# A hybrid diffusion layer on one core: constant matmuls ahead of the first ff tile, PSUM sums copied by ScalarE, weight loads released one by one, lo parts last

## The chip, the cores and the metric

The kernel runs on one core of a Trainium2 chip. The metric is device time in microseconds (us). A core has TensorE for matmuls (PE in the profile; its weight loads are PEld), VectorE (DVE), ScalarE (ACT), GpSimd (POOL) and SyncE (SP). Loads from HBM are asked for by instructions on a queue, SP's, POOL's or ACT's, and are carried by 16 DMA engines.

## The reference

One layer over 256 latent tokens and 256 context tokens of width 2048: a half-step SwiGLU, a mixing step (grouped-query attention beside a Hyena long convolution), and a second half-step SwiGLU for the latent tokens. Each is RMS-normed and modulated by a linear map of the conditioning vectors.

```python
mod = (s_lat @ w_ada[l] + b_ada[l])[:, None, :]          # 9 chunks of 2048; s = silu(c)
mod_c = (s_ctx @ w_ada[l] + b_ada[l])[:, None, :]        # the same for the context
def half_ffn(s, m, slot, g, w_up, w_down):
    h = rms_norm(s, g) * (1 + chunk(m, 3*slot + 1)) + chunk(m, 3*slot)
    return s + 0.5 * chunk(m, 3*slot + 2) * swiglu(h, w_up, w_down)
x = half_ffn(x, mod, 0, g_norm[l, 0], w_ffn1_up[l], w_ffn1_down[l])        # and ctx with mod_c
...
h = (h @ w4).reshape(L, 2, HYENA_WIDTH) * exp(-t * abs(decay))             # the Hyena filter's taps
kk = concat([h[:, 0], zeros, h[:0:-1, 1]]); kk = kk / sum(abs(kk), axis=0)
x = x + chunk(mod, 5) * merge_groups(attention(...), hyena(..., kk), g_out[l], w_out[l])
x = half_ffn(x, mod, 2, g_norm[l, 2], w_ffn2_up[l], w_ffn2_down[l])
```

## The kernel before

Everything is kept transposed: a tile holds 128 of the 2048 channels (KT = 16 such d) by 256 tokens, latent and context side by side (i = 0, 1), so one matmul has 512 columns. For precision each factor is split into a hi part (a cast to fp32r by ScalarE) and a lo part (what the cast lost, by VectorE), and a product takes three matmuls: whi with the input's hi, whi with its lo, wlo with its hi (`mm3`, L232 to L234; L221 and L225 make the weights' parts).

The change lies in the first 165 us. There three ff tiles (WAVE = 3, j = 0 to 2) are summed up at the same time, channel block by channel block, because the modulation of block d is only just being made. For each d:

- `row_on(d + 1)`, `ada_row` (L175): row sums of w_ada for block d + 1, 32 small matmuls in four column groups over two wrow tiles of 1 MB (the halves kh). A row block's tiles are loaded on SP's queue by `row_load` (L162), two blocks ahead; four buffers hold them.
- `ada_col` (L182 to L190): ScalarE copies the sums out of their PSUM bank (L182), TensorE transposes them (L184), VectorE reduces them to columns of scale and shift, `mod` (L187 to L190).
- `wave_h` (L657 to L661; for d = 0 and 1 `times_rs` and `wave_h_early`, L637 and L644 to L649): normed input times scale plus shift, hi by ScalarE and lo by VectorE.
- the three tiles' matmuls, `f1.tile(d, d % 4, w[j], wave[j])`.
- after d = 3, 7, 11 the next weights: `weights_on` casts raw to whi and wlo (L221, L225). The raw tiles of 512 KB (`raws`, L209) come on POOL's queue.
- one step of `filter_spectrum`, the Hyena filter, a generator that is moved on by one `next(steps)` after each tile. Its four rounds q each load taps on POOL's queue (`load_taps`: L425, L428), make them (L465 to L492), sum their magnitudes (psn: L495, L496; reciprocal L498, middle bin L499) and transform them (L504 to L507). L509 to L512 write the result to DRAM.

The bank of PSUM that a row block, a transform or the sums of magnitudes use comes from one pool of four (`PB`, "pb" in the rows); two of the four hold the third ff tile all through this stage.

Ahead of d = 0 stand the sums of squares of the tokens (L596 and the matmuls of 2 columns), the row sums of block 0 and the spreading of 1/rms over the partitions (row, two matmuls of 512 columns at 21.79 us in the profile). `keep_awake(n)` issues n constant matmuls (ones by a tile of ones, 256 columns, L583) whose result nobody reads: 17 at the start and 5 after the first half of the sums.

A planner lays out each engine's order from the program's order and its own estimates of when operands are ready. `then(x, f, ...)` and `tc.issue_after(x)` hold f behind x in that order. Two places before the change:

```python
gate = G.tensor_copy(warm, mod[0][0][:, d : d + 1])
with tc.issue_after(gate.ins):
    raws = [weight_load(f1.wup[j, d // 4 + 1], (P, 4, 2, P), G) for j in range(WAVE)]
```

Of the kernel before, what the change touches and what calls it, by code (L numbers as in the profile page):

```python
# [18 lines left out]
P = 128  # L19
D = 2048  # L20
KT = D // P
# [10 lines left out]
WAVE = 3  # L32
# [1 line left out]
FILTER_J = 36  # L34
GATE_J = 20

AWAKE = (17, 5)

QSTEP = (2, 1, 3, 2)
FILL = (2, 0)  # L40
# [15 lines left out]
def hybrid_layer_kernel(ctx: ExitStack, tc: tile.TileContext, a):  # L56
    nc = tc.nc
    V, S, G, PE = nc.vector, nc.scalar, nc.gpsimd, nc.tensor
# [56 lines left out]
    mod = [[None] * 9, [None] * 9]  # L115
# [7 lines left out]
    warm = mod[0][8][:, 0:1]  # L123
# [83 lines left out]
    def weight_load(src, shape, queue=None):  # L207
        raw = T(wp, shape, "raw", bufs=4)
        load = (queue or nc.sync).dma_start(raw, src)  # L209
        loads.append(load)  # L210
        if done[0]:
            last_load[0] = load
        return raw
# [38 lines left out]
    def then(behind, do, *args, **kw):  # L252

        with tc.issue_after(behind.ins):
            return do(*args, **kw)
# [87 lines left out]
    class Ffn:  # L343
# [18 lines left out]
        def tile(self, k, k4, w, ps2):  # L362
            for half in range(2):
                mm = self.mm(ps2[half], (w[0][:, k4, half, :], w[1][:, k4, half, :]), self.h[k], k == 0, k == KT - 1)
            return mm

        def close(self, j, ps2):
            sg = tmp2((P, 2, L))
            S.activation(sg, ps2[0], AF.Silu)
            V.tensor_mul(sg, ps2[1], sg)  # L370
            self.acts[j] = split(sg, (P, 2, L))
# [40 lines left out]
    def filter_spectrum():  # L412
# [47 lines left out]
        for q in range(4):  # L460
            now = taps.pop()
            if q < 3:
                taps.append(load_taps(q + 1))
            dec, w4 = now
            S.activation(dec, dec, AF.Abs)  # L465
            kts, pm = [], []
            for t in range(2):
                kts.append(U((P, 2, L)))
                S.activation(kts[t], dec, AF.Exp, scale=tneg[:, t : t + 1])
            whi, wlo = U((P, 2, L), F32R), U((P, 2, L), F32R)  # L470
            S.copy(whi, w4)
            V.tensor_sub(wlo[0:NF], w4[0:NF], whi[0:NF].bitcast(F32))
            yield
            yield
            for t in range(2):
                ps, ht = PB((P, 2, L)), hid[:, t * P : (t + 1) * P]
                PE.matmul(ps, ht, whi, start=True, stop=False)
                PE.matmul(ps, ht[0:NF], wlo[0:NF], start=False, stop=True)
                V.tensor_mul(kts[t], ps, kts[t])
            V.memset(kts[0][0:1, 1, :], 0.0)  # L480
            yield
            for kt in kts:
                pm_ = U((P, 2, L))
                V.tensor_add(pm_[:, 0, :], kt[:, 0, :], kt[:, 1, :])
                V.tensor_sub(pm_[:, 1, :], kt[:, 0, :], kt[:, 1, :])
                pm.append(pm_)
            yield
            for kt in kts:
                S.activation(kt, kt, AF.Abs)
            ab = kts[0][:, 0, :]  # L490
            V.tensor_add(kts[0], kts[0], kts[1])
            V.tensor_add(ab, ab, kts[0][:, 1, :])  # L492
            yield
            psn = PB((P, 2, L))
            PE.matmul(psn[:, 0, :], ones, ab, start=True, stop=True)  # L495
            PE.matmul(psn[0:1, 1, :], alt, pm[0][:, 0, :], start=True, stop=True)  # L496
            rn, mid = T(up, (P, L), "mt", bufs=3), T(up, (1, L), "mt", bufs=3)
            V.reciprocal(rn, psn[:, 0, :])  # L498
            V.tensor_mul(mid, psn[0:1, 1, :], rn[0:1, :])  # L499
            yield  # L500
            for sn in range(2):
                ps, eo, o = PB((P, 2, L)), kts[sn], now[sn]
                for t in range(2):
                    PE.matmul(ps[:, t, :], mats[:, sn, t, :], pm[t][:, sn, :], start=True, stop=True)  # L504
                V.tensor_mul(eo, ps, rn.unsqueeze(1).broadcast_to((P, 2, L)))
                V.tensor_add(o[:, 0, :], eo[:, 0, :], eo[:, 1, :])
                V.tensor_sub(o[:, 1, :], eo[:, sn, :], eo[:, 1 - sn, :])  # L507
                if sn:
                    V.tensor_copy(o[0:1, 0, :], now[0][0:1, 1, :])  # L509
                    V.tensor_copy(now[0][0:1, 1, :], mid)  # L510
                    for n in range(2):
                        nc.gpsimd.dma_start(spec[2 * q + n], now[n])  # L512
                yield
                if not sn:
                    yield
# [38 lines left out]
    f1 = Ffn(a["w_up1"], a["w_dn1"], 0)  # L554
    load = then(load, row_load, 0)

    raws = [T(wp, (P, 4, 2, P), "raw", bufs=4) for _ in range(WAVE)]
    w = {j: tuple(T(wp, (P, 4, 2, P), n, F32R, 3) for n in ("whi", "wlo")) for j in range(WAVE)}
# [17 lines left out]
    def keep_awake(n, behind=None, bank=spin):  # L576

        last = behind
        with ExitStack() as order:
            if behind is not None:  # L580
                order.enter_context(tc.issue_after(behind.ins))
            for _ in range(n):
                last = PE.matmul(bank[:, 0 : 2 * P], ones, pair, start=True, stop=True)  # L583
        return last
# [9 lines left out]
    for n, t in enumerate(xs[0] + xs[1]):  # L594
# [14 lines left out]
        for i, sq in reversed(summed):  # L609
            for tt in range(2):  # L610
                for j in range(2):
                    awake = then(awake, PE.matmul, sums[:, 2 * i + tt, :], sq[:, j, tt * P : (tt + 1) * P], ones[:, 0:2],
                                 start=n == 7 and (tt, j) == (0, 0), stop=sq is acc and n == 15 and (tt, j) == (1, 1))
        summed, last = [], awake
# [2 lines left out]
    root_table(square)  # L617
    vector(V.tensor_scalar, bada1, bada[:, KT : 2 * KT], 1.0, None, ALU.add)
    r_ = token_root(sums, D)
    for half in range(2):  # L620
        last = then(last, ada_row, 0, (half,))

    parts, row = T(up, (P, 2, 4), "mt", F32R, bufs=3), PB((P, 2, L))
    V.tensor_copy(parts[:, 0, :], r_)
# [42 lines left out]
    wave = [f1.open(alt=j >= 2) for j in range(WAVE)]  # L667
# [6 lines left out]
    spread = S.copy(rs, row)  # L674
    with tc.issue_after(scaled.ins):
        copied, turned_, bank = then(spread_last, ada_col, 0)
    with tc.issue_after(copied.ins), tc.issue_after(made_lo.ins):
        shifted, lo_last = wave_h_early(0)

# [17 lines left out]


    scaled = then(lo_last, times_rs, 1, rs)
    mm = f1.tile(0, 0, w[0], wave[0])  # L700
    mm = then(mm, row_on, 1)
    mm = then(mm, f1.tile, 0, 0, w[1], wave[1])
    with tc.issue_after(mm.ins), tc.issue_after(scaled.ins), tc.issue_after(shifted.ins):
        copied, mm, _ = ada_col(1)
# [3 lines left out]
    mm = then(mm, f1.tile, 0, 0, w[2], wave[2])  # L708
# [12 lines left out]
    for d in range(1, KT):  # L721
        if d > 1:
            mm = then(mm, row_on, d + 1) or mm
        for j in range(WAVE):
            mm = then(mm, f1.tile, d, d % 4, w[j], wave[j])
            if d == 1 and j == 0:
                mm = then(mm, row_on, 2)
            if (d, j) != (1, 0):
                next(steps, None)
            if j == (1 if d == 1 else 0):  # L730
                mm = then(mm, col_on, d + 1) or mm
            weights_on(d, j)
        if d % 4 == 1 and d // 4 < 3:
            gate = G.tensor_copy(warm, mod[0][0][:, d : d + 1])
            with tc.issue_after(gate.ins):
                raws = [weight_load(f1.wup[j, d // 4 + 1], (P, 4, 2, P), G) for j in range(WAVE)]
    for _ in steps:
        pass
    ahead = weight(f1.wup[WAVE, 0], (P, 4, 2, P))
# [290 lines left out]
    gate = gate_steps()  # L1030
# [169 lines left out]
    for b in range(NB):  # L1200
# [4 lines left out]
        ps, last = out_unit(1, b, 3 if final else 1)  # L1205
# [9 lines left out]
    with tc.issue_after(last.ins):  # L1215
        for _ in range(AWAKE2):
            last = PE.matmul(spin[:, 0:P], ones, ones, start=True, stop=True)
# [61 lines left out]
    for g in range(UPG):  # L1279
# [12 lines left out]
        for kp in range(8):  # L1292
# [8 lines left out]
            for k2 in range(2):  # L1301
                k = 2 * kp + k2
# [153 lines left out]
```

## Time and profile before

| | |
|---|---|
| time, median of 3 runs | 2654.93 us (2654.65 to 2655.61) |
| the profiled execution | 2655.01 us |
| its span, first to last instruction | 2653.2 us |
| TensorE busy | 2632.3 us, 99% |
| VectorE busy | 1723.7 us, 65% |
| ScalarE busy | 942.2 us, 36% |
| DMA | 515.78 MB, 194 GB/s over the span |

The profile is of one execution. Its times count from the first instruction. "Idle before, releaser" gives how long an engine stood idle ahead of an instruction and what ended that. Some lines stand under the line of a helper: L255 is `then`. A matmul's end is modelled, and matmuls overlap, so the pace of TensorE is read from starts.

### The profile page before, as it was taken

How to read it: one execution, taken by the hardware profiler on the slowest of the kernel's cores; microseconds unless marked ns; L12 is line 12 of the kernel's file. 1: busy time of each engine (PE TensorE's matmuls, PEld its weight loads, DVE VectorE, ACT ScalarE, POOL GpSimd, SP SyncE). 2: the span in 40 equal slices, each digit the busy share in tenths (PEclk: the TensorE clock that was granted, in tenths of full speed). 3: DMA queues.
4: the chain of work that ended last, by engine and by line, in shares of the span. 5: the costliest groups of instructions: out<-in, count | busy, mean ns of one | idle time of the engine just before them, and what ended most of it. 6: DMA issues, size and time to landing. Idle time of an engine off the chain costs nothing.

```text
span 2653.2 us, 32468 instructions
## 1 busy us (share of the span) xinstructions
PE 2632.3 (99%) x12482; PEld 2167.3 (82%) x12482; DVE 1723.7 (65%) x2707; ACT 942.2 (36%) x1242; POOL 21.2 (1%) x44
## 2 busy tenths in 40 slices
PE   8999999999999999999999999999999999999999
PEld 5678888888888888888888988888788888888887
DVE  6789899976696666533333696889665555554444
ACT  5333222222222222222222465456554444444333
POOL 1100000000000000000000000000000000000000
PEclk8999999999999999999999999999999999999999
DMA  9976656565686565632222455335555555556664
GB/s 364 364 247 213 217 209 235 207 233 211 229 286 244 203 228 213 212 98 101 95 96 95 134 173 195 126 129 164 169 184 189 191 190 191 189 188 206 202 201 157
DMA packets 143575, 515.78 MB, mean 194 GB/s; under 512 B 16699, under 2 KB 19708, under 8 KB 139068
## 3 DMA queue, kind: packets, MB, share of 16 engines
q1 hardware_dynamic: 140012, 501.77, 55.1%
q0 software_dynamic: 2784, 9.18, 1.0%
q10 hardware_dynamic: 624, 2.75, 0.3%
q8 instruction: 98, 1.61, 0.2%
q14 instruction: 57, 0.47, 0.0%
HBM read 509.43 MB, written 4.21 MB: 194 GB/s over the span
## 4 chain that ended last, share of the span: by engine, by line
PE 97%; DMA 1%; DVE 1%; ACT 0%; issue 0%; SPq 0%; DVEq 0%; ACTq 0%
PE pa L232 12%; PE pa L233 12%; PE pa L234 12%; PE pa L1119 10%; PE pa L1120 10%; PE pa L1118 10%; PE pb L232 7%; PE pb L233 7%; PE pb L234 7%; PE pa L240 3%; PE pa L242 2%; PE pb L175 1%; PE pa L832 1%; PE pa L833 1%; PE pa L831 1%; DMA wrow<-in_w_ada_dram 1%
## 5 line engine op out<-in xcount | busy, mean ns | idle before, releaser
L225 DVE TENSOR_TENSOR wlo<-raw,whi 128x1024 fp32r<-128x1024 f32 x639 | 781.2, 1223 | 634.3 <-ACT whi L221 623.1
L221 ACT CAST whi<-raw 128x1024 fp32r<-128x1024 f32 x639 | 672.2, 1052 | 1330.2 <-PE pa L233 473.7
L232 PE MATMUL pa<-u,whi 128*128 128x512 f32 x1376 | 538.3, 392 | 2.1 <-ACT u L644 2.1
L233 PE MATMUL pa<-u,whi 128*128 128x512 f32 x1376 | 536.2, 390 | 0.4 <-DVE u L649 0.4
L234 PE MATMUL pa<-u,wlo 128*128 128x512 f32 x1376 | 535.9, 390 | 0.0
L1118 PE MATMUL pa<-whi,u 128*128 128x512 f32 x1060 | 413.9, 391 | 0.0
L1119 PE MATMUL pa<-wlo,u 128*128 128x512 f32 x1060 | 412.8, 390 | 0.2 <-DVE wlo L225 0.2
L1120 PE MATMUL pa<-whi,u 128*128 128x512 f32 x1060 | 412.8, 390 | 0.0
L232 PEld LDWEIGHTS pa<-u,whi 128*128 128x128 f32 x1376 | 258.2, 188 | 61.6 <-issue 4.5
L233 PEld LDWEIGHTS pa<-u,whi 128*128 128x128 f32 x1376 | 258.5, 188 | 54.3 <-DVE u L649 1.5
L234 PEld LDWEIGHTS pa<-u,wlo 128*128 128x128 f32 x1376 | 258.5, 188 | 53.9
L232 PE MATMUL pb<-u,whi 128*128 128x512 f32 (+1 forms) x800 | 299.5, 375 | 0.0
L233 PE MATMUL pb<-u,whi 128*128 128x512 f32 (+1 forms) x800 | 297.8, 372 | 0.0
L234 PE MATMUL pb<-u,wlo 128*128 128x512 f32 (+1 forms) x800 | 297.7, 372 | 0.0
L1119 PEld LDWEIGHTS pa<-wlo,u 128*128 128x128 f32 x1060 | 199.1, 188 | 41.4 <-DVE wlo L225 0.6
L1120 PEld LDWEIGHTS pa<-whi,u 128*128 128x128 f32 x1060 | 199.0, 188 | 41.3
L1118 PEld LDWEIGHTS pa<-whi,u 128*128 128x128 f32 x1060 | 199.0, 188 | 40.7
L138 DVE CUSTOM_DVE_ANT_0 adas<-adaw,crow,mod 128x1024 bf16<-128x1024 f32 x160 | 205.2, 1282 | 28.4 <-DMA adaw<-in_w_adaT_dram 25.7
L138 DVE CUSTOM_DVE_ANT_0 adas<-adaw,crow,cond 128x1024 bf16<-128x1024 f32 x160 | 204.9, 1280 | 20.4 <-DMA adaw<-in_w_adaT_dram 18.6
L232 PEld LDWEIGHTS pb<-u,whi 128*128 128x128 f32 x800 | 150.6, 188 | 28.2 <-issue 2.1
L233 PEld LDWEIGHTS pb<-u,whi 128*128 128x128 f32 x800 | 150.7, 188 | 26.4 <-issue 0.4
L234 PEld LDWEIGHTS pb<-u,wlo 128*128 128x128 f32 x800 | 150.7, 188 | 26.3
(290 smaller groups left out, 2131.4 us busy)
## 6 DMA issues: line engine op xcount, KB each, us to landing
raw<-in_w_up_dram SPq DMA_DIRECT2D x340, 512.0 KB, 3.3
adaw<-in_w_adaT_dram SPq DMA_DIRECT2D x223, 512.0 KB, 5.0
raw<-in_w_dn_dram SPq DMA_DIRECT2D x184, 512.0 KB, 4.1
wrow<-in_w_ada_dram SPq DMA_DIRECT2D x32, 1024.0 KB, 9.4
raw<-in_w_hy_dram SPq DMA_DIRECT2D x32, 512.0 KB, 3.3
raw<-in_w_o_dram SPq DMA_DIRECT2D x32, 512.0 KB, 3.4
raw<-in_w_kv_dram SPq DMA_DIRECT2D x16, 512.0 KB, 3.6
raw<-in_w_q_dram SPq DMA_DIRECT2D x16, 512.0 KB, 3.3
```

Of the source, the lines that this page charges most:

```text
L138: V.tensor_tensor_reduce(out=sc, in0=t, in1=crow[i][:, b * (D // 2) : (b + 1) * (D // 2)], scale=1.0, scalar=mcol if b else bada[:, n : n ...
L175: last = PE.matmul(bank[g : g + 32, 0 : 2 * P], cs[:, k, :], t[:, k8, :], start=k < 4, stop=k >= KT - 4)
L221: S.copy(hi, raw)
L225: V.tensor_sub(lo, raw, hi.bitcast(F32))
L232: PE.matmul(ps, w[0], xx[0], start=start, stop=False)
L233: PE.matmul(ps, w[0], xx[1], start=False, stop=False)
L234: return PE.matmul(ps, w[1], xx[0], start=False, stop=stop)
L240: PE.matmul(ps, w[0], x, start=start, stop=stop)
L242: PE.matmul(ps[:, 0, :], w[1], x[:, 0, :], start=False, stop=False)
L1118: PE.matmul(ps[t], hi, w[0], start=start, stop=False)
L1119: PE.matmul(ps[t], hi, w[1], start=False, stop=False)
L1120: last = PE.matmul(ps[t], lo, w[0], start=False, stop=stop)
```

## The change

Five edits. `AWAKE` gets two more numbers: one constant matmul between the halves of row block 0, and three behind the transposes of `ada_col(0)`, written to the half of that bank that has been copied. `tile_late` takes the products with the input's lo part last; it is used for the first of the three tiles of each d. In the filter, ScalarE copies both sums out of PSUM, and VectorE works on the copies. The three weight loads of a group are no longer issued together behind column d at the end of d = 1, 5, 9: the first is issued in tile j = 2 of that d behind column d + 1, the second and third in tiles 0 and 2 of the next d (2, 6, 10) behind that d's column d + 1.

```diff
-AWAKE = (17, 5)
+AWAKE = (17, 5, 1, 3)
...
+        def tile_late(self, k, k4, w, ps2):
+
+            hi, lo = self.h[k]
+            for part in (0, 1):
+                for half in range(2):
+                    PE.matmul(ps2[half], w[part][:, k4, half, :], hi, start=k + part == 0, stop=False)
+            for half in range(2):
+                mm = PE.matmul(ps2[half], w[0][:, k4, half, :], lo, start=False, stop=k == KT - 1)
+            return mm
...
-            V.reciprocal(rn, psn[:, 0, :])
-            V.tensor_mul(mid, psn[0:1, 1, :], rn[0:1, :])
+            S.copy(rn, psn[:, 0, :])
+            S.copy(mid, psn[0:1, 1, :])
+            V.reciprocal(rn, rn)
+            V.tensor_mul(mid, mid, rn[0:1, :])
...
-    for half in range(2):
-        last = then(last, ada_row, 0, (half,))
+    last = then(last, ada_row, 0, (0,))
+    last = keep_awake(AWAKE[2], last)
+    last = then(last, ada_row, 0, (1,))
...
         copied, turned_, bank = then(spread_last, ada_col, 0)
+    keep_awake(AWAKE[3], turned_, bank)
...
-    mm = f1.tile(0, 0, w[0], wave[0])
+    mm = f1.tile_late(0, 0, w[0], wave[0])
...
-            mm = then(mm, f1.tile, d, d % 4, w[j], wave[j])
+            mm = then(mm, f1.tile if j else f1.tile_late, d, d % 4, w[j], wave[j])
...
-        if d % 4 == 1 and d // 4 < 3:
-            gate = G.tensor_copy(warm, mod[0][0][:, d : d + 1])
-            with tc.issue_after(gate.ins):
-                raws = [weight_load(f1.wup[j, d // 4 + 1], (P, 4, 2, P), G) for j in range(WAVE)]
+            if d < KT - 4 and (d % 4, j) in ((1, 2), (2, 0), (2, 2)):
+
+                gate = G.tensor_copy(warm, mod[0][0][:, d + 1 : d + 2])
+                at = d % 4 - 1 + j // 2 * (d % 4 - 1)
+                raws[at] = then(gate, weight_load, f1.wup[at, d // 4 + 1], (P, 4, 2, P), G)
```

## Rows read from the trace of the kernel before

**Rows 1.** The page: TensorE's busy time and share of the span, its granted clock and the busy share of the DMA engines, in tenths, in 40 slices of 66 us.

```profile
PE 2632.3 (99%) x12482; PEld 2167.3 (82%) x12482; DVE 1723.7 (65%) x2707; ACT 942.2 (36%) x1242; POOL 21.2 (1%) x44
...
PEclk8999999999999999999999999999999999999999
DMA  9976656565686565632222455335555555556664
```

**Rows 2.** What TensorE waited for from 10 to 165 us: us in total, how often, the longest.

```profile
PE pb L175 <- DMA wrow<-in_w_ada_dram: 2.9, 3, 1.2
PE pb L175 <- DVE mt L499: 2.8, 3, 1.7
PE pa L232 <- ACT u L644: 2.1, 1, 2.1
...
PE pb L175 <- DVE u L479: 0.5, 1, 0.5
PE pa L233 <- DVE u L649: 0.4, 1, 0.4
```

**Rows 3.** Stretches of the head: us, then busy us and instructions of PE, PEld, DVE, ACT, POOL, then the granted clock, the DMA engines' share and GB/s.

```profile
18.00:31.00 13.00, 10.11 (x62) 4.53 (x58) 6.84 (x21) 3.06 (x7) 0.00 (x0) 0.50 1.01 388
...
31.50:34.50 3.00, 3.00 (x20) 2.16 (x13) 0.53 (x3) 1.03 (x4) 0.00 (x0) 1.00 1.03 429
```

**Rows 4.** TensorE in order of time around the first tiles: start and length in us, line, operation, out<-in, count, and the idle time before.

```profile
19.93 1.93 PE L175 MATMUL pb<-wrow,csp 128*32 128x256 f32 x16 [0.81 <-DMA wrow<-in_w_ada_dram]
21.79 1.22 PE L255 MATMUL pb<-u,u 128*128 128x512 f32 x2
...
25.52 1.22 PE L232 MATMUL pa<-u,whi 128*128 128x512 f32 x2 [2.08 <-ACT u L644]
...
28.71 3.23 PE L175 MATMUL pb<-wrow,csp 128*32 128x256 f32 x32
31.87 0.50 PE L232 MATMUL pa<-u,whi 128*128 128x512 f32 x1
...
33.50 0.48 PE L232 MATMUL pb<-u,whi 128*128 128x512 f32 x1
...
37.90 1.93 PE L175 MATMUL pb<-wrow,csp 128*32 128x256 f32 x32
...
51.90 1.07 PE L175 MATMUL pb<-wrow,csp 128*32 128x256 f32 x16 [0.86 <-DMA wrow<-in_w_ada_dram]
...
60.54 1.07 PE L175 MATMUL pb<-wrow,csp 128*32 128x256 f32 x16 [1.20 <-DMA wrow<-in_w_ada_dram]
```

**Rows 5.** VectorE in order of time ahead of the first tile.

```profile
22.12 0.42 DVE L570 TENSOR_TENSOR wlo<-raw,whi 128x256 fp32r<-128x256 f32 x1 [0.40 <-ACT whi L567]
23.05 0.75 DVE L637 TENSOR_TENSOR u<-u,pb 128x256 f32<-128x256 f32 x2 [0.51 <-PE pb L255]
```

**Rows 6.** The DMA engines from 40 to 60 us: two stretches with the columns of rows 3; then SP's queue (q1) and POOL's (q0) from 40 to 50 us, with packets, MB and share; then two issues, with their count, KB each and the median us to landing, of the same 10 us and of the next.

```profile
40.00:50.00 10.00, 10.00 (x72) 6.74 (x71) 8.11 (x26) 4.54 (x9) 3.92 (x8) 1.00 0.98 349
50.00:60.00 10.00, 8.48 (x71) 4.92 (x70) 5.31 (x16) 4.33 (x7) 1.08 (x2) 1.00 1.03 345
...
q1 hardware_dynamic: 289, 2.13, 52.3%
q0 software_dynamic: 383, 1.35, 45.5%
...
u<-in_fdft_dram POOLq DMA_DIRECT2D x1, 256.0 KB, 15.7
...
u<-in_flt_w_dram POOLq DMA_DIRECT2D x2, 128.0 KB, 12.4
```

**Rows 7.** The sums of magnitudes and the bank they hold, in order of time: TensorE and VectorE at 98 to 102 us, then TensorE, VectorE and ScalarE at 124 to 128 us; last, ScalarE's group of copies of 128x256 out of PSUM (count, busy us, mean ns).

```profile
98.47 0.59 PE L496 MATMUL pb<-u,u 128*1 128x256 f32 x2
...
99.56 1.03 PE L504 MATMUL pb<-u,u 128*128 128x256 f32 x4
101.53 0.42 PE L175 MATMUL pb<-wrow,csp 128*32 128x256 f32 x4 [0.94 <-DVE mt L499]
...
99.10 1.76 DVE L498 RECIPROCAL mt<-pb 128x256 f32<-128x256 f32 x1 [0.33 <-PE pb L496]
...
101.08 0.41 DVE L499 TENSOR_TENSOR mt<-pb,mt 1x256 f32<-1x256 f32 x1
...
127.22 0.42 PE L175 MATMUL pb<-wrow,csp 128*32 128x256 f32 x4 [1.71 <-DVE mt L499]
...
125.69 1.16 DVE L225 TENSOR_TENSOR wlo<-raw,whi 128x1024 fp32r<-128x1024 f32 x1
...
124.46 1.04 ACT L221 CAST whi<-raw 128x1024 fp32r<-128x1024 f32 x1 [0.80 <-PE pb L233]
...
L182 ACT COPY sg<-pb 128x256 f32<-128x256 f32 x16 | 5.9, 372 | 35.0 <-PE pb L175 35.0
```

**Rows 8.** The second group of weights: the three loads of raw on POOL's queue (issue times) and their us to landing; then VectorE's last step of column 7, and ScalarE's third cast and the copy behind it.

```profile
L209 POOL DMA_DIRECT2D raw<-in_w_up_dram x3: 530/553/582, 64.9 to 66.0; - x3
...
DMA to landing us min/median/max: 8.5/11.7/16.1
...
80.72 0.22 DVE L190 TENSOR_SCALAR mod<-col,cond 128x2 f32<-128x2 f32 x1
...
91.89 1.05 ACT L221 CAST whi<-raw 128x1024 fp32r<-128x1024 f32 x1 [1.35 <-PE pb L233]
...
94.07 0.37 ACT L182 COPY sg<-pb 128x256 f32<-128x256 f32 x1 [1.14 <-PE pb L175]
```

## The prediction

> **What bounds the kernel now.** I read the page first. TensorE is busy in 99% of the span, so its idle time is at most some 21 us, and the slices of its clock show one more loss: the first slice is below full speed [rows 1]. DMA is busy nine tenths or more in the first two slices only. So two places can give anything: TensorE's idle stretches, and the head, where the clock is down and the DMA engines are full. Then I asked for TensorE's waits from 10 to 165 us, the stretch that holds every edit. Most of its waits there are of two kinds: the row sums of the modulation (L175) wait 2.9 us for their weights wrow and 2.8 us for a product made of PSUM by VectorE (L499); 2.1 us stand before the first ff tile [rows 2]. Third, the clock by stretches: 0.50 from 18 to 31 us, half of full speed (1.2 of 2.4 GHz), although TensorE was busy in 10.1 of these 13 us, and 1.00 from 31.5 [rows 3]. After 165 us TensorE waits a few times for some tenths, far from the edits, so what the head gives or loses should be shifted through to the end.
>
> **Constant matmuls.** One call of the helper (a matmul of 256 columns in two passes) goes into the gap ahead of the second half of row block 0, three calls into the gap ahead of the first tile. At half clock a matmul pass of 512 columns takes about 0.43 us (six from 25.52 to 28.71, with 0.4 us of waiting for the lo part); these passes, fp32 at 256 columns, I take at the same. Two passes are 0.86 us in a gap of 0.81; six are 2.6 us in the gap that begins after the transposes of L184 and ends at 25.52 [rows 2, 4]. If the clock stays down they overrun by some 0.5 us, or by 1.0 if they must wait for VectorE's read of the same bank. If they bring the clock back before the first tile, three things shrink. The first tile: 3.2 us (25.52 to 28.71) becomes at most the 1.6 us that the second tile took at full clock (31.87 to 33.50, two transposes in it). Row block 1: 3.2 us (28.71 to 31.87) becomes 1.9 (the row at 37.90). The two matmuls at 21.79 get shorter, but VectorE's last lo split before them ends at 22.54 and L637 starts at 23.05 now, so at most 0.5 us of that arrives [rows 4, 5]. Together up to 1.6 + 1.3 + 0.5 = 3.4 us of TensorE time; from below, minus 1.0.
>
> **Lo parts last.** The first tile of each d takes the two hi products and the wlo products before the lo ones. The number of matmuls and weight loads is the same. It covers the wait of L233 for u (0.4 us once in [rows 2], and about as much inside the first tile, which the 3.4 already holds). I count 0.4 at most and 0 at least.
>
> **Weight loads released one by one.** Before, three loads of 512 KB go out on POOL's queue at the end of d = 1, 5, 9, all gated by column d, which is done one step earlier. Now the first waits for column d + 1 and the other two for column d + 2, so they leave about one and two steps later; the gates are POOL copies of 128x1 that nobody waits for. What is this worth? The two waits that it can remove are those of row blocks 4 and 5, 0.9 and 1.2 us, together 2.1 [rows 2, 4]. With the clock that makes 3.4 + 2.1 = 5.5 us as the upper bound of the front, if the rows then landed as early as TensorE wants them.
>
> They won't, I think. From 40 to 50 and from 50 to 60 us the DMA engines are at shares of 0.98 and 1.03, moving 349 and 345 GB/s, for SP's queue (rows) and POOL's (weights, filter taps) together. A TensorE that reaches row block 4 or 5 earlier waits there longer, unless bytes leave the stretch. The weights themselves can't leave it: they are cast for d = 4, right after row block 5. What can be pushed behind the rows is what POOL issues after them in the program: the DFT matrices (256 KB) and the second set of taps (four of 128 KB), 0.79 MB, or 2.3 us at 345 GB/s; two of the tap loads, issued at about 50 us and 12.4 us on their way, had not landed by 60 us anyway [rows 6]. So I take 1.5 us for the whole front (clock, lo parts and release together), nearer to the DMA bound than to the 5.5; the ends are 0 and 5.5.
>
> The Trainium skill ("Trainium Kernel Development and Optimization", Key Constraints) says that DMAs of the SP, ACT and POOL queues run on the same 16 engines and interleave. By that rule alone a later release moves no byte away, the front gives 0 instead of 1.5, and the sum below would be 2652.5. The shares near 1.00 with both queues at work agree with it.
>
> **Sums copied out of PSUM by ScalarE.** The bank of psn now is held until the reciprocal (1.75 us) and L499 (0.41) have read it, and the next row block needs the bank: at 99.06 the sums are there, at 101.49 L499 is done, and L175 starts at 101.53 after 0.94 us of idling. At d = 12 another split (L225) slips between the two and the wait is 1.71 us; the third is 0.2 [rows 2, 7]. Two ScalarE copies of at most 0.372 us each (a 128x256 copy out of PSUM, the nearest row) free the bank 0.75 us after the sums, at about 99.8, before TensorE has done the four matmuls that stand ahead of L175. So the waits at 76 and 101 go. At d = 12 ScalarE casts weights at that time, the last one from 124.46 to 125.5; if the copies are planned behind it the bank is free at 126.2, where L175 now starts at 127.22, so 1.0 of 1.7 is sure. I take 2.5 us, of 2.1 to 2.8. The added 0.75 us ahead of the reciprocal delays L505, for which TensorE doesn't wait in any of the four steps; if it did, the price would be 4 x 0.75 = 3.0 us, which is the lower end. No row shows a reciprocal of this size from SBUF; I keep 1.75 us.
>
> **The sum.** 1.5 + 2.5 = 4.0 us. The profiled execution took 2655.01 us (span 2653.2, 1.8 around it), which is 0.1 us from the median of 2654.93, so 2651.0 us. That is 0.15% less: within the 0.2% (5.3 us) that a measurement of this kernel can tell from no change.
>
> **Rivals.**
> Rows in time. If the loads held back let the rows through (POOL's queue has less to move while row blocks 4 and 5 are on their way), the front gives its 5.5 and the bank 2.8: 2655.0 - 8.3 = 2646.7. For it: the first release waits for one column more, and until it comes SP's queue has the engines to itself; from 40 to 50 us POOL's queue moved 1.35 MB beside SP's 2.13 [rows 6]. Against: the same weights are due for d = 4 as before, and the engines were full before too.
>
> Bytes don't move. The front gives nothing, by the engines' shares of rows 6 (this is the page's rule as a mechanism), the bank 2.5: 2652.5. Half of this case lies inside my likeliest range.
>
> ScalarE waits for late weights (slower). ScalarE works in order, and the cast of a weight (L221) that has not landed holds the copy L182 that TensorE's transposes need. In the second group the loads went out at 64.9 to 66.0 and the slowest took 16.1 us; two of them would now leave after column 7, at about 81. Landing at 97 instead of 82, the third cast (at 91.89 now) would end at 98.1 and L182, at 94.07 now, start 4 us late. Less some slack on TensorE, that is 3 us or so a group, 9 us for three; with 4.0 gained it ends at 2660.0. It decides once a load takes over 12 us (94.07 less 1.05 for the cast less 81). Against it: the shortest in that group took 8.5, and now two compete instead of three. The first tap loads stand in the same POOL queue and could be late in the same way [rows 8].
>
> The bank is no bound: another wait of VectorE's takes its place (L479 holds a bank for 0.5 us already [rows 2]) and the clock stays down: 2655 to 2656.
>
> **How the numbers follow.** The forecast, DMA-bound front and freed bank, 0.45; it runs from 2648 to 2654 (front from minus 1.0, the overrun of the constant matmuls, to 4.0; bank 2.1 to 2.8). Rows in time 0.22; bytes don't move 0.10; ScalarE late 0.13; no bound 0.10. Faster by over 0.2% needs less than 2649.6: all of the second case and a tail of 0.11 of the first, 0.33. Slower by over 0.2% is above 2660.2: most of the late case and nothing else, 0.12 with what the replanned order may add. Same, 0.55. The range reaches from 2645.8 (the second case with the 0.4 of the lo parts and 0.5 of L479) to 2657.5 (half of the late case's price).
>
> **What would show it.** Clock: 1.00 before 28 us, the first tile at some 1.5 us. Front: waits of L175 for wrow that stay or grow (over 2.9 us in total) if I am right; gone, and row block 6 more than 4 us earlier than 67.84, if the second case is. Bank: no wait of L175 for L499, copies of 0.37 us by ScalarE right after L496. Late case: ScalarE's L221 or L465 waiting for DMA raw or flt_decay by several us, and L184 waiting for sg. I am wrong in the mechanism if DMA falls well below a share of 1.0 between 40 and 60 us, or if TensorE's time after 165 us changes by itself by more than 1 us.

## The result, and the profile of the changed kernel

The changed kernel takes 2666.84 us (median of 6 runs, 2666.12 to 2668.51) against 2654.52 of the kernel before (6 runs beside it, 2654.01 to 2655.61). The ratio is 1.0047, 95% interval 1.0034 to 1.0059: slower by 12.3 us, where I had forecast 4 us faster and a range that ended at 2657.5. The profiled execution took 2667.11 us, 12.1 more than that of before.

The page of after, its first line and TensorE's:

```profile
span 2665.3 us, 32503 instructions
...
PE 2636.6 (99%) x12490; PEld 2171.6 (81%) x12490; DVE 1726.0 (65%) x2707; ACT 943.9 (35%) x1250; POOL 22.6 (1%) x50
```

Against [rows 1] TensorE is busy 4.3 us longer (2636.6 less 2632.3) with 8 matmul passes more, those of the constant matmuls; the span before was 2653.2, so its idle time grew from 20.9 to 28.7 us, by 7.8. Two parts of the loss, then: new waits, and work that runs slower. The lines have moved: L372 and L374 are the matmuls of `tile_late`, L672 stands where L659 stood, L475 where L465 stood, L435 and L438 are the tap loads, L749 is the gate. What TensorE waited for from 10 to 175 us (us in total, times, longest):

```profile
PE pa L372 <- ACT u L672: 9.0, 1, 9.0
PE pb L184 <- ACT sg L182: 5.2, 2, 3.0
...
PE pa L372 <- DVE wlo L582: 0.7, 1, 0.7
...
PE pb L175 <- DMA wrow<-in_w_ada_dram: 0.3, 1, 0.3
```

The two waits that the change was to remove are gone: wrow 2.9 to 0.3, and L499's 2.8 to nothing [rows 2]. In their place stand three long waits for ScalarE: one of 9.0 us for the h of the tile of d = 4 (L672), which follows row block 5, two for the copy L182 (3.0 and 2.2). The clock by stretches (us; busy us and instructions of PE, PEld, DVE, ACT, POOL; granted clock, DMA share, GB/s):

```profile
19.20:22.60 3.40, 3.13 (x22) 1.10 (x18) 2.71 (x8) 1.20 (x3) 0.00 (x0) 0.51 1.01 366
22.60:60.10 37.50, 33.38 (x260) 20.31 (x256) 21.99 (x64) 11.97 (x25) 7.03 (x14) 1.00 1.01 396
60.20:70.40 10.20, 4.07 (x11) 3.19 (x12) 4.33 (x9) 7.31 (x12) 0.60 (x1) 0.50 0.96 307
97.70:101.10 3.40, 3.40 (x8) 1.63 (x6) 3.40 (x8) 1.86 (x4) 0.00 (x0) 0.51 1.02 423
125.00:128.40 3.40, 3.40 (x9) 2.06 (x7) 1.80 (x6) 0.91 (x2) 1.49 (x4) 0.51 1.02 424
```

The clock is at its upper level from 22.6 us, not from 31.4 [rows 3]. But it falls to half three times more: during the first of the new waits, and 0.9 and 0.4 us after the end of the other two (96.8 and 124.6 us). The work in these three stretches (4.07, 3.40 and 3.40 us at half clock) would take half as long at full clock, so I estimate that they cost 5.4 us.

When the row blocks of the modulation begin (the first L175 of each d, us in the trace; then the differences to before, negative is earlier; e1, e2 and e7 are runs told of below):

| row block | before | after | after | e1 | e2 | e7 |
|---|---|---|---|---|---|---|
| d = 2 | 37.9 | 36.0 | -1.9 | -2.0 | -2.4 | -2.0 |
| d = 5 | 58.3 | 55.4 | -2.9 | -0.7 | -3.5 | -3.0 |
| d = 6 | 67.8 | 74.5 | +6.7 | -0.6 | +8.3 | +1.4 |
| d = 8 | 83.8 | 90.3 | +6.5 | -0.8 | +8.3 | +1.2 |
| d = 9 | 92.0 | 103.2 | +11.1 | -0.9 | +12.8 | +2.7 |
| d = 10 | 101.5 | 111.6 | +10.1 | -2.0 | +12.7 | +1.6 |
| d = 11 | 108.9 | 119.0 | +10.1 | -2.0 | +12.7 | +1.6 |
| d = 12 | 117.0 | 131.0 | +14.0 | +0.3 | +15.4 | +1.6 |
| d = 13 | 127.2 | 139.5 | +12.3 | -1.5 | +15.4 | +0.2 |
| d = 15 | 142.7 | 155.0 | +12.2 | -1.5 | +15.4 | +0.2 |

Read downwards, after gains 2.9 us up to d = 5 and then loses in three steps, behind d = 5, 8 and 11. Where TensorE waited for 9.0 us ScalarE did this (start, us, line, operation, out<-in, and the idle time before with what ended it), and below it the later rounds of the filter:

```profile
51.79 1.05 ACT L221 CAST whi<-raw 128x1024 fp32r<-128x1024 f32 x1 [1.17 <-PE pa L374]
62.65 0.63 ACT L475 ACTIVATE u<-u 128x512 f32<-128x512 f32 x1 [9.81 <-DMA u<-in_flt_decay_dram]
63.19 1.98 ACT L221 CAST whi<-raw 128x1024 fp32r<-128x1024 f32 x2
65.07 0.41 ACT L455 ACTIVATE u<-mt 128x256 f32<-128x256 f32 x1
65.39 0.89 ACT L672 ACTIVATE u<-sq,mod 128x256 fp32r<-128x256 f32 x2
...
95.88 0.63 ACT L475 ACTIVATE u<-u 128x512 f32<-128x512 f32 x1 [5.42 <-DMA u<-in_flt_decay_dram]
96.42 0.35 ACT L182 COPY sg<-pb 128x256 f32<-128x256 f32 x1
...
123.69 0.63 ACT L475 ACTIVATE u<-u 128x512 f32<-128x512 f32 x1 [4.58 <-DMA u<-in_flt_decay_dram]
```

ScalarE stands for 9.81 us at L475, the absolute value of a round's filter taps, until the tap load lands. Two casts, L455 and the L672 that TensorE needs are behind it in ScalarE's order. At 95.88 and 123.69 the same instruction holds up the copy L182. So the question is why the taps are late. POOL's queue, first of after, then the same loads of before, with ScalarE's first use of them as the last line:

```profile
40.59 0.28 POOL L749 COPY mod<-mod 128x1 f32<-128x1 f32 x1 [38.83 <-DVE mod L190]
41.15 0.68 POOL L209 DMA_DIRECT2D raw<-in_w_up_dram  x1 [0.27 <-issue]
46.63 0.29 POOL L749 COPY mod<-mod 128x1 f32<-128x1 f32 x1 [4.80 <-DVE mod L190]
47.21 0.54 POOL L209 DMA_DIRECT2D raw<-in_w_up_dram  x1 [0.28 <-issue]
47.74 0.25 POOL L749 COPY mod<-mod 128x1 f32<-128x1 f32 x1
47.93 0.53 POOL L209 DMA_DIRECT2D raw<-in_w_up_dram  x1
48.45 1.07 POOL L435 DMA_DIRECT2D u<-in_flt_decay_dram  x2
...
59.36 0.61 POOL L438 DMA_DIRECT2D u<-in_flt_w_dram  x1 [3.66 <-DMA raw<-in_w_up_dram]
...
88.62 1.07 POOL L435 DMA_DIRECT2D u<-in_flt_decay_dram  x2
...
117.25 1.07 POOL L435 DMA_DIRECT2D u<-in_flt_decay_dram  x2
```

```profile
39.75 1.10 POOL L425 DMA_DIRECT2D u<-in_flt_decay_dram  x2
...
66.50 1.08 POOL L425 DMA_DIRECT2D u<-in_flt_decay_dram  x2
...
99.58 1.08 POOL L425 DMA_DIRECT2D u<-in_flt_decay_dram  x2
...
53.37 0.64 ACT L465 ACTIVATE u<-u 128x512 f32<-128x512 f32 x1
```

The gates (L749) wait on POOL for a column of the modulation, and POOL works in order, so what the program issues behind them waits too. The first taps went out at 39.75 before and go out at 48.45 now; those of the later rounds 22.1 and 17.7 us later, of which 6.5 and 10.1 us are TensorE's own delay by then (row blocks 8 and 10 in the table). Of the first round the slower of the two decay loads landed at 52.5 before, 0.9 us ahead of its use at 53.37; now it lands at 62.6.

The taps are not the only load that is late. The third weight of this group, issued at 47.93, was 11.1 us on its way and landed at 59.0 (POOL's 59.36 above). Had ScalarE not stood at the taps, it would have stood for this weight, and with the durations above (one cast, L455, L672) TensorE could have gone on at about 61.4 us instead of 66.33. By this estimate some 4 of the 9.0 us are the weights' and 5 the taps'.

### The profile page after: what moved, and what is told of

The parts are those of the page before. It is cut to its first block, busy times and chain, and to the rows that moved or that the text cites. A ratio compares the mean times of both kernels' runs of the same rounds, so it can differ in the third digit from the quotient of the medians.

```text
span 2665.3 us, 32503 instructions
## 1 busy us (share of the span) xinstructions
PE 2636.6 (99%) x12490; PEld 2171.6 (81%) x12490; DVE 1726.0 (65%) x2707; ACT 943.9 (35%) x1250; POOL 22.6 (1%) x50
## 4 chain that ended last, share of the span: by engine, by line
PE 96%; DMA 2%; DVE 1%; ACT 1%; issue 0%; SPq 0%; POOL 0%; POOLq 0%; ACTq 0%; DVEq 0%
PE pa L232 11%; PE pa L233 11%; PE pa L234 11%; PE pa L1134 10%; PE pa L1133 10%; PE pa L1135 10%; PE pb L232 7%; PE pb L233 7%; PE pb L234 7%; PE pa L240 3%; PE pa L242 2%; PE pa L847 1%; PE pa L848 1%; PE pa L846 1%; PE pb L175 1%; DMA u<-in_flt_decay_dram 1%
## 5 line engine op out<-in xcount | busy, mean ns | idle before, releaser
L221 ACT CAST whi<-raw 128x1024 fp32r<-128x1024 f32 x639 | 672.1, 1052 | 1342.0 <-PE pa L233 471.4
L232 PE MATMUL pa<-u,whi 128*128 128x512 f32 x1344 | 525.4, 391 | 0.0
L233 PE MATMUL pa<-u,whi 128*128 128x512 f32 x1344 | 524.2, 390 | 0.0
L234 PE MATMUL pa<-u,wlo 128*128 128x512 f32 x1344 | 524.1, 390 | 0.0
L234 PEld LDWEIGHTS pa<-u,wlo 128*128 128x128 f32 x1344 | 253.0, 188 | 52.7
L232 PEld LDWEIGHTS pa<-u,whi 128*128 128x128 f32 x1344 | 252.8, 188 | 52.7 <-issue 0.8
L233 PEld LDWEIGHTS pa<-u,whi 128*128 128x128 f32 x1344 | 252.9, 188 | 51.9
L138 DVE CUSTOM_DVE_ANT_0 adas<-adaw,crow,mod 128x1024 bf16<-128x1024 f32 x160 | 205.2, 1282 | 20.3 <-DMA adaw<-in_w_adaT_dram 17.7
```

Source lines behind the costliest of these rows:

```text
L138: V.tensor_tensor_reduce(out=sc, in0=t, in1=crow[i][:, b * (D // 2) : (b + 1) * (D // 2)], scale=1.0, scalar=mcol if b else bada[:, n : n ...
L221: S.copy(hi, raw)
L232: PE.matmul(ps, w[0], xx[0], start=start, stop=False)
L233: PE.matmul(ps, w[0], xx[1], start=False, stop=False)
L234: return PE.matmul(ps, w[1], xx[0], start=False, stop=stop)
```

## The experiments

All but e2 and e4 start from the changed kernel. The explanation I set out with (A in the expectations) is the one above: the gates push the tap loads back, and ScalarE's order passes that on to TensorE. The rivals were, above all, that the weights themselves are late (C) and that with full DMA engines each load moved ahead only delays another (D). Medians stand against about 2654.8 us of the kernel before on the same chip (24 to 27 runs).

| run | median us | ratio | 95% interval |
|---|---|---|---|
| e1_release_old | 2653.42 | 0.9996 | 0.9987 to 1.0005 |
| e2_release_only | 2674.38 | 1.0072 | 1.0059 to 1.0084 |
| e3_taps_first | 2658.12 | 1.0013 | 1.0004 to 1.0022 |
| e4_copies_only | 2654.92 | 1.0003 | 0.9994 to 1.0011 |
| e5_taps_gated | 2661.33 | 1.0026 | 1.0016 to 1.0037 |
| e6_taps_gated_release_old | 2656.81 | 1.0008 | 0.9999 to 1.0017 |
| e7_taps_sp | 2655.83 | 1.0004 | 0.9996 to 1.0013 |
| e8_gap_filled | 2668.83 | 1.0053 | 1.0039 to 1.0067 |
| e9_abs_later_release_old | 2653.51 | 0.9995 | 0.9986 to 1.0004 |
| e10_abs_later_taps_sp | 2658.47 | 1.0012 | 1.0003 to 1.0021 |
| e11_abs_later | 2664.86 | 1.0035 | 1.0022 to 1.0047 |
| e12_front_only | 2655.75 | 1.0001 | 0.9993 to 1.0010 |

**e1 and e2: the release taken back, and alone.** e1 is the changed kernel with the old release; e2 is the kernel before with the new release and nothing else.

```diff
-            if d < KT - 4 and (d % 4, j) in ((1, 2), (2, 0), (2, 2)):
-                gate = G.tensor_copy(warm, mod[0][0][:, d + 1 : d + 2])
-                at = d % 4 - 1 + j // 2 * (d % 4 - 1)
-                raws[at] = then(gate, weight_load, f1.wup[at, d // 4 + 1], (P, 4, 2, P), G)
+        if d % 4 == 1 and d // 4 < 3:
+            gate = G.tensor_copy(warm, mod[0][0][:, d : d + 1])
+            with tc.issue_after(gate.ins):
+                raws = [weight_load(f1.wup[j, d // 4 + 1], (P, 4, 2, P), G) for j in range(WAVE)]
```

> The kernel after, with the weight loads released as in the kernel before (three together behind column d); the constant matmuls, the lo parts last and ScalarE's copies stay. Theory A (the release puts the filter's tap loads behind the new gates in POOL's queue, ScalarE waits for them in order and TensorE with it): the waits of 9.0, 3.0 and 2.2 us are gone, and what is left of the change is a gain: about 2650 us, 2648 to 2653. Rival B (the order that the planner makes of the other edits is what costs): stays at 2662 or more. Rival C (the weights' own late landing is the whole loss, taps play no part): like A here, about 2650; e3 tells it from A.

> The kernel before with the new release of the weight loads alone. Theory A: ScalarE's step L465 waits for flt_decay by about 10, 5 and 5 us, TensorE stands by about 9, 3 and 2 us and its clock falls after each; without the gain of the other edits 2666 to 2672 us. Rival B: within 3 us of before, 2652 to 2658. Rival C: 2666 to 2672 too, but ScalarE's waits are for raw, not for flt_decay.

e1: 2653.42 us, the whole loss gone. Its longest waits of TensorE, its DMA waits of ScalarE, and its first tap loads:

```profile
PE pb L175 <- DMA wrow<-in_w_ada_dram: 3.1, 3, 1.3
PE pb L184 <- ACT sg L182: 2.0, 1, 2.0
...
ACT u L475 <- DMA u<-in_flt_decay_dram: 4.9, 2, 4.4
...
37.45 1.10 POOL L435 DMA_DIRECT2D u<-in_flt_decay_dram  x2
```

e2: 2674.38 us, 19.6 us slower than before:

```profile
PE pa L232 <- ACT u L659: 11.3, 1, 11.3
PE pb L184 <- ACT sg L182: 5.3, 2, 2.8
...
ACT u L465 <- DMA u<-in_flt_decay_dram: 18.8, 3, 8.7
ACT whi L221 <- DMA raw<-in_w_up_dram: 4.7, 1, 4.7
```

The release by itself makes the loss, in the same places. The two runs don't add up: e1's -1.4 and e2's +19.6 give 18.2, after lost 12.3. Half of these 6 us is the execution: the profiled one of e2 was its fastest (2671.53), and between the profiled executions 2.8 us are left. Of these TensorE's three long waits for ScalarE hold 2.4: 16.6 us in e2, 14.2 in after, with ScalarE standing 4.7 us for a weight in e2. The rest I have not traced; the order that the planner writes differs in each kernel. e1 also shows the price of the old release at the front: the waits for wrow are back (3.1 us).

**e4 and e12: the other parts alone.** e4 is the kernel before with ScalarE's copies only; e12 is it with the constant matmuls and the lo parts last only.

```diff
-            V.reciprocal(rn, psn[:, 0, :])
-            V.tensor_mul(mid, psn[0:1, 1, :], rn[0:1, :])
+            S.copy(rn, psn[:, 0, :])
+            S.copy(mid, psn[0:1, 1, :])
+            V.reciprocal(rn, rn)
+            V.tensor_mul(mid, mid, rn[0:1, :])
```

> The kernel before with ScalarE's copies of the sums of magnitudes alone. My step on the bank: the three waits of L175 for L499 (2.8 us) go, 2652.0 us, between 2651.5 and 2652.8. If the bank is no bound (another wait takes its place): 2654 to 2655.

> The kernel before with the constant matmuls and the lo parts last, without ScalarE's copies and with the old release. My step on the DMA bound: row block 1 ends 2 to 3 us earlier, row blocks 4 and 5 wait longer for wrow, and at row block 6 under 1 us of it is left: 2654 us, 2653.5 to 2655. If the front's gain were kept: 2651 to 2652.

e4: 2654.92, no change. No wait for VectorE's product is left, but others took its place (TensorE's two longest that are new or grown, and ScalarE's):

```profile
PE pb L175 <- DMA wrow<-in_w_ada_dram: 3.9, 3, 1.9
...
PE pb L184 <- ACT sg L182: 1.9, 1, 1.9
...
ACT u L465 <- DMA u<-in_flt_decay_dram: 5.7, 2, 4.4
```

ScalarE comes to the taps of the last round at 108.9 us, as before (109.0), but they land later (113.2 for the slower load, 110.7 before), and the clock is at half from 60.4 to 63.8 and from 115.0 to 118.4. e12: 2655.75, no change in the median; the profiled execution, its fastest (2652.64), has all row blocks from d = 6 on 2.0 us earlier, with 2.2 us of waits for wrow. So neither part has a gain that can be measured by itself.

**e7: the taps on another queue.** The changed kernel, the tap loads issued by SP.

```diff
-                nc.gpsimd.dma_start(dec[:, fb, :],
+                nc.sync.dma_start(dec[:, fb, :],
...
-                nc.gpsimd.dma_start(w4[r * NF : (r + 1) * NF],
+                nc.sync.dma_start(w4[r * NF : (r + 1) * NF],
```

> The kernel after with the filter's taps asked for on SP's queue instead of POOL's, at the same places of the program; the release one by one stays. Theory A: ScalarE's waits for flt_decay of 10, 5 and 5 us go, or shrink to what the place behind the rows in SP's queue costs (0 to 3 us each); below 2660, most likely 2650 to 2655. If POOL's queue is not the cause (contention of the engines is): the waits stay as long and the time stays at 2664 or more.

2655.83 us: 11.0 of the 12.3 are back, with the same bytes, the same gates and the same release.

```profile
PE pa L372 <- ACT u L672: 4.2, 1, 4.2
...
ACT u L475 <- DMA u<-in_flt_decay_dram: 9.8, 4, 5.0
ACT whi L221 <- DMA raw<-in_w_up_dram: 3.8, 3, 1.7
```

The first tap load is issued at 43.70 and ScalarE's longest wait falls from 9.8 to 5.0 us. So most of the loss goes with the taps' place in POOL's queue. e7 changes the queue as well as the place and doesn't tell the two apart. The 4.2 us that TensorE still waits at the tile of d = 4 are still the taps': ScalarE stands for them until 57.7, and the third weight landed at 56.0.

**e3, e5 and e6: the taps moved ahead.** e3 issues them some steps earlier in the program. e5 puts them behind gates of their own (rounds 0 and 1 behind column 1, the others behind columns 5 and 8) and the weights' gates behind the last tap load; e6 is e5 with the old release. The core of e5:

```diff
+            gate = G.tensor_copy(warm, mod[0][0][:, behind : behind + 1])
+            with tc.issue_after(gate.ins):
...
-            if li == 1:
-                taps = [load_taps(0)]
+            if li == 0:
+                taps = [load_taps(0, 1), load_taps(1, 1)]
...
-                gate = G.tensor_copy(warm, mod[0][0][:, d + 1 : d + 2])
+                gate = then(last_tap[0], G.tensor_copy, warm, mod[0][0][:, d + 1 : d + 2])
```

> The kernel after, with each set of taps asked for some steps earlier in the program, so that the loads stand ahead of the gates of their group in POOL's queue; nothing else is changed. Theory A: ScalarE no longer waits for flt_decay, the 9.0 us wait of TensorE goes, and the time is that of e1 or a little less, 2647 to 2653 us. Rival C: the waits turn into waits for raw (weights landing behind the taps) and the time stays above 2660. Rival B: stays at 2662 or more.

> The kernel after, with the order in POOL's queue set: the taps of rounds 0 and 1 leave behind column 1 and the weights of the first group behind them, one by one as in the kernel after; the taps of round 2 behind column 5, of round 3 behind column 8. Theory A (only the taps' place in POOL's queue made the loss): no wait of ScalarE for flt_decay over 1 us, no clock of 0.5 after 30 us, row block 6 at 66 us or earlier, 2648 to 2651 us. Rival C (the weights, released later, are themselves late): waits of ScalarE for raw take the place, 2655 or more. Rival D (the DMA engines are the bound of this stretch, so what is moved ahead delays what is moved behind): the waits of L175 for wrow grow to 3 us or more, 2652 to 2655.

> As the run before, but with the weights of a group together behind their taps and the old column, as in the kernel before. What the release one by one is worth once the taps are out of its way: theory A 1 to 2 us slower than the run before (2650 to 2652), as the rows of block 4 and 5 wait again for 2 to 3 us. Rival D: the same as the run before within 1 us, since the same bytes pass the engines by block 5.

e3: 2658.12. The planner put the first taps at 1.7 us, among the loads of x, and row block 0 began 6.0 us later (`PE pb L255 <- DVE u L255` 5.2 us); most of that was made up by d = 5 (+1.0). At the tile of d = 4 a wait of 3.9 us stayed, and behind it ScalarE stood for weights and not for taps (L221 for `raw`, 2.37 us at 59.1 and 2.74 at 62.9; its first wait for taps comes at 84.2): a sign of C. The time lies between what I expected under A (2653 at most) and under C (over 2660), and as e3 moved the delay as well as the taps, it prices neither.

e5: 2661.33, e6: 2656.81. With the taps ahead, the 9.0 us wait is 2.1 in e5 (two waits), but the weights for row block 4 landed at 49.3 and 52.9 instead of 44.2 and 47.6, the waits for wrow are 2.9 us, and ScalarE still waits 8.1 us for later taps. What is moved ahead delays what is behind it: D holds here. The Trainium skill ("Trainium Kernel Development and Optimization", Key Constraints) says that DMAs of the three queues run on the same 16 engines and interleave; for SP's and POOL's queues these runs agree, with the weights for row block 4 landing 5.1 and 5.3 us later. And e5 is 4.5 us slower than e6, where I had expected e6 to be the slower one: the new release costs even where no tap load stands behind a weight's gate. The two part at row block 10 (8.9 us behind the kernel before in e5, 6.8 in e6), ahead of which ScalarE stands 4.63 us for the last taps in e5 and 1.80 in e6; the slower of these loads was 8.0 us on its way in e5 and 5.3 in e6.

**e9, e10 and e11: the use of the taps moved back.** The absolute value of the taps is held behind the last L182 (two steps later in round 0), in e1, in e7 and in the changed kernel.

```diff
-            S.activation(dec, dec, AF.Abs)
+            if q == 0:
+                yield
+                yield
+            then(last_copied[0], S.activation, dec, dec, AF.Abs)
```

> The kernel with the old release and the other three edits (the first experiment), and in it the filter's first ScalarE step on each set of taps (the absolute value of flt_decay) held behind the latest copy L182, with round 0 two steps later. Theory A (what eats the gain there is ScalarE standing in order for flt_decay, 4.4 us, of which TensorE gets 2.0): that wait goes, 2651 us, 2650 to 2652. If other waits take its place again: 2653 to 2655.

> The kernel after with the taps on SP's queue and the absolute value held as in the run before. Theory A: the release one by one keeps its 2 to 3 us up to row block 5, the 5.0 us wait for flt_decay no longer stops TensorE: 2649 us, 2647 to 2651. If late weights (waits for raw, 3.8 us with the taps on SP's queue) are a loss of their own: 2652 to 2655.

> The kernel after, with nothing but the absolute value held later as in the two runs before; the taps stay behind the gates on POOL's queue and land as late as in the kernel after. Theory A in its sharpest form (not the late landing, but ScalarE standing in order for it, is what stops TensorE): the 9.0 us wait shrinks to 3 us or less, 2652 to 2658. If the late landing by itself costs it (the steps behind it are needed as soon): 2662 or more.

e9: 2653.51; e10: 2658.47; e11: 2664.86. Under A I expected 2651 of e9 and 2649 of e10, and both missed: in e9 other waits stand in the place of the one that went (3.2 us for wrow, 1.2 and 0.9 for VectorE), and e10 is 2.6 us slower than e7. A in its sharpest form, that only ScalarE's standing at the taps costs, falls with e11, where ScalarE waits 0.2 us in all for taps and 10.0 us of the loss stay. Against e9, which has the same filter and the old release, it is 11.4 us slower. TensorE's two longest waits in e11, then two lines of ScalarE's order of time:

```profile
PE pb L184 <- ACT sg L182: 7.3, 1, 7.3
PE pa L372 <- ACT u L675: 5.1, 1, 5.1
...
59.20 1.04 ACT L221 CAST whi<-raw 128x1024 fp32r<-128x1024 f32 x1 [3.81 <-DMA raw<-in_w_up_dram]
...
132.52 1.04 ACT L221 CAST whi<-raw 128x1024 fp32r<-128x1024 f32 x1 [10.30 <-DMA raw<-in_w_up_dram]
```

With ScalarE no longer standing at the taps, the weights themselves are late and hold ScalarE in the same manner: C is true as well, behind A. At the tile of d = 4 TensorE now goes on at 61.41, where the estimate above put it. In e10, where the taps are off the queue, the casts still wait 9.4 us in all. With the old release (e9) ScalarE has no DMA wait at either line. So the release delays both loads that ScalarE works on, and which of them it waits for first depends on the order.

**e8: the first gap filled.** To price the clock, 19 constant matmuls between row block 5 and the tile of d = 4.

```diff
+            if (d, j) == (4, 0):
+                for _ in range(19):
+                    mm = then(mm, PE.matmul, ada_bank[5][:, 2 * P : 4 * P], ones, pair, start=True, stop=True)
```

> The kernel after with 19 more constant matmuls (8 us at full clock) between row block 5 and the tile of d = 4 that waits 9.0 us. What the clock's fall costs on top of the wait: the wait itself stays (ScalarE's 9.8 us for flt_decay are untouched), but the clock is 1.00 from 60 to 70 us, row block 6 comes 2 us earlier than in the kernel after (72.5 instead of 74.5), and the time is 2664 to 2666. If the clock's fall costs nothing: unchanged, 2666 to 2668.

2668.83 us, not faster. The clock stayed up to 72.3 us and the first tile's wait is 1.0, but ScalarE's order was planned anew: the copy L182 now stood behind another tap wait, and row block 6 began at 77.8 (74.5 in after). TensorE's longest waits, then the added passes in TensorE's order of time:

```profile
PE pb L184 <- ACT sg L182: 10.3, 3, 4.4
PE pa L372 <- ACT u L672: 1.0, 1, 1.0
...
56.03 8.47 PE L255 MATMUL pb<-u,ones 128*128 128x256 f32 x38
```

The price of the clock's fall is not settled by this; the 5.4 us above are worked out from durations, not shown by a run.

## Why the prediction was wrong

**The step that failed** is the one on the release: "the gates are POOL copies of 128x1 that nobody waits for". They cost POOL some 0.3 us each, but POOL stands at them, and everything that it issues behind them stands too. I named the second taps, which stand behind the weights in the program, and booked their delay as relief for the rows. I did not walk through POOL's queue in the trace of before, where the first taps follow the three weight loads directly (issued at 39.75) and land 0.9 us ahead of their use. An issue that moves by 8.7 us against a margin of 0.9 is a loss, and that sum could be made blind. The weights behind the gates are late too, and hold ScalarE as soon as the taps don't (10.30 us in e11); with the taps on SP's queue and the absolute value held back 3.6 us of loss are left (e10).

**The relief was real.** Rows did come in time: 1.9 us were gained by row block 2, 2.9 by row block 5, and the 1.2 us wait inside row block 5 [rows 4] is gone too, 4.1 us in all: 1.9 for the head and 2.2 for the rows, all that my second case gave them. That is nearer to its 5.5 than to the 1.5 that I took. With the old release 2.3 us (e12) or 0.7 (e1) are left at row block 5, and the waits for wrow stay. The rows gain in just the stretch where the taps lose:

```profile
40.00:50.00 10.00, 10.00 (x91) 6.03 (x89) 6.03 (x21) 2.91 (x7) 4.05 (x9) 1.00 0.98 387
50.00:60.00 10.00, 7.34 (x58) 4.63 (x54) 4.84 (x14) 1.42 (x2) 2.98 (x6) 1.00 1.02 384
```

The DMA engines were as full as before (shares 0.98 and 1.02; 0.98 and 1.03 before), but they moved 387 and 384 GB/s instead of 349 and 345 [rows 6], and SP's queue 5.69 MB in these 20 us instead of 4.62. So the second step that failed is "nearer to the DMA bound": a share near 1.0 did not bound the bytes at 345 GB/s, and [rows 3] had already shown 429 GB/s at a share of 1.03. The term is 4.1 us where I took 1.5. Why more was moved at the same share is not shown; POOL's queue moved 1.99 MB instead of 2.31.

**The sum by the trace.** Gains: the front's 4.1, and at row blocks 7, 10 and 13 the bank's 0.2, 1.0 and 1.7, together 7.0. Losses: the waits of 9.0, 3.0 and 2.2, together 14.2, and 5.4 for the clock, 19.6. The difference, 12.6, stands against 12.1 between the two profiled executions.

**Clock at the head.** Right that it comes back before the first tile (from 22.6 us), and that the row then takes 1.9 us. That the constant matmuls do it is likely: with them the head is at half clock for 3.4 us (after, e1, e5, e6, e8, e9, e11, e12), not at all (e7, e10), or, where the row sums began late, for 6.7 (e3); without them it is 13.7 (before), 10.3 (e4) and twice some 3.4 (e2). With one trace of each kernel, and such a spread, it is not shown. The 3.4 us of gain were too many: the first tile begins 0.35 us later than before (25.87), row block 1 1.0 us earlier, row block 2 1.9 earlier, with a new wait of 0.7 us for VectorE's lo part in between (L372 for L582).

**Bank.** Right in mechanism and size inside this kernel: two copies of 0.37 and 0.36 us, the three waits for L499 gone, 2.9 us at row blocks 7, 10 and 13 against my 2.5; the reciprocal from SBUF took 1.75 us, as I had kept. But alone (e4) it gives nothing, since TensorE then waits for rows and taps that don't come earlier. I had counted it as kept to the end.

**The slower rival** had the engine and the chain right (ScalarE in order behind a late load, L182 behind it), and its last sentence named the taps. I priced it at 3 us a group for a weight that lands late, gave it 0.13 and left the clock out. Measured it is 9.0, 3.0 and 2.2 us of waiting and 2.0, 1.7 and 1.7 of clock behind them. "Bytes don't move" and "no bound" fell: the front gave 4.1 us, and the bank's waits went.

**Slips in the working.** The six passes from 25.52 to 28.71, less 0.4, give 0.47 us each at half clock and not 0.43. The 2657.5 of the range is not half of the late case's price (9 us) but half of what the gains leave of it (5 us). After 165 us the longest wait of TensorE before is 1.2 us, not some tenths; nothing came of it, as the loss at row block 15 (12.2 us) is that of the whole (12.1).

What stays open: the price of the clock's fall as a measured number; the shares of the taps and of the weights in the loss, beyond the estimate for the first wait; what is left of the 6 us by which e1 and e2 don't add up; whether an order of POOL's and SP's loads exists that keeps the rows' gain without the taps' loss. The fastest medians, e1 and e9, are 1.3 to 1.4 us below the kernel before with intervals that include 1, so no version here is shown to beat it.

## What to carry to other kernels

A wait added to an engine that also issues loads is a wait added to every load behind it: list the queue from the trace in order, with each load's margin between landing and use, before the gate is priced at nothing. An engine that works in order passes one late operand on to all that is planned behind it, so the price is that of the most urgent instruction behind, not of the one that waits. Where the DMA engines are full, relief for one stream is delay for another; ask which of the two has the smaller margin.

## What the runs showed of the hardware

Three things I had not expected. Small loads took long among many others: the 128 KB tap loads issued on POOL from 40 to 56 us took a median of 14.6 us to landing, and 6.7 and 5.8 us where fewer loads were on their way (issued at 88.6 and 117.3). By the fit in the Trainium skill ("DMA: Bandwidth & Descriptors", Anatomy of one DMA) such a load would be estimated at 2.3 us; no run here shows one alone, and the shortest of those loads in e5, at 70.4 us, took 3.2. POOL also paused between its tap loads until earlier loads had landed (3.33, 3.66 and 1.10 us at 55.2, 59.4 and 61.1; 1.40, 4.68 and 0.92 us in the kernel before). Counted from issues and landings, eight loads of POOL's queue were under way at each of these six pauses; whether the program or the queue sets that number is not shown. And the clock fell to half after a wait of TensorE as short as 1.9 us (e4, the waits that end at 60.1 and 114.2 us), with TensorE at work before and after it, and stayed there for 3.4 us of full work; yet it did not fall after 1.99 us in e1 (112.4) and 2.48 in e2 (127.6), so that a wait of this length does not foretell it.
